# Linear ReLU attention on one core: K and V four heads to a tile in place of eight

## Chip, core and metric

The kernel runs on one NeuronCore of a Trainium2 chip. The metric is device time in microseconds, the median over several executions of the same program. One more execution was taken with the hardware profiler; its own time stands beside its span below, and every duration in this document comes from such a profiled execution.

The engines are named as in the profile: PE (TensorE, with its weight loads as PEld), DVE (VectorE), ACT (ScalarE), POOL (GpSimd) and SP (SyncE). Loads that turn float32 into bfloat16 are issued by POOL, plain transfers by SP and ACT; all of them run on the same 16 DMA engines.

## What is computed

Batch 8, 12 heads, sequence 512, head size 64, everything float32 in HBM (96 heads in all, 12.58 MB for each of Q, K, V and the output).

```python
Q_feat = np.maximum(0, Q)
K_feat = np.maximum(0, K)
KV = np.einsum('bhkd,bhkv->bhdv', K_feat, V)
K_sum = np.sum(K_feat, axis=2)
numerator = np.einsum('bhqd,bhdv->bhqv', Q_feat, KV)
denominator = np.einsum('bhqd,bhd->bhq', Q_feat, K_sum)
return (numerator / (denominator[:, :, :, None] + 1e-10)).astype(np.float32)
```

Each head first reduces K and V to a 64x64 matrix `KV` (with `K_sum` as a 65th column), and then every row of Q is multiplied by it and divided by its denominator.

## The kernel before, in words

**Tiling.** Eight heads make an octet (`o`, 0 to 11). Q and the output of an octet are 1 MB of float32 each, 128 partitions of 32 rows, so one head lies on 16 partitions. In octets 1 to 10, K and V are laid out the same way: one 1 MB load for K and one for V (`load_kv`, lines 99 to 105), 8 KB of float32 for each partition. The step number `g` = 2·o + i then means half of each partition's rows (16 of 32), of all eight heads. Octets 0 and 11 (`by4`, line 37) use another layout: there `g` means four of the eight heads, 32 partitions to a head, 16 rows to a partition, and each K or V load is 512 KB (`load_kv4`, lines 93 to 97; for octet 0 lines 112 to 116, float32, by SP and ACT).

**Keeping heads apart.** One matmul contracts over all 128 partitions, so the heads that share them are kept apart by masks. `prep(g)` (lines 171 to 186) writes K twice, times a mask for even and for odd heads (`kf`, two DVE instructions that also do the ReLU), and V once for each pair of heads (`vo`). With eight heads there are four pairs, so V is written four times (`NT = 4`): three on DVE and one on ACT for an even `g`, two and two for an odd one. With four heads there are two pairs: one copy on DVE, one on ACT. A 65th column of `vo`, set once for each buffer (`ones8`, `ones4`), holds ones in the partitions of the pair and gives `K_sum`.

**K times V.** `mm_kv(g)` (line 188) runs 16 matmuls, one for each row of a partition, with 128 columns of `kf` as weights and 260 columns of `vo` moving (four pairs of 65), or 130 with four heads. With eight heads the two steps of an octet add into one PSUM tile, and `evac_kv` (line 200) copies it on ACT after the second step, in four copies of 64x260 into `kvd`. With four heads each step has its own PSUM tile and four copies of 64x130.

**Q.** `qt(o)` transposes the octet's Q on PE (16 transposes) and ACT writes it back with the ReLU (`evac_qt`, four instructions). `out_round(o, j)`, three to an octet, multiplies it with `kvd` (`mm_out`) and DVE divides (`norm`: `den`, `rec`, `o_sb`).

**Order.** The order on every engine is written out by hand (lines 277 to 340), and each engine takes its instructions in that order. In iteration `o` of the loop: step `kv(2o)`, round 0 of octet o-1, `prep(2o+2)`, round 1, `kv(2o+1)`, `qt(o)`, `prep(2o+3)`, round 2, store of octet o-1. The last octets differ: in iteration 10 `prep(22)` stands behind all rounds of octet 9; in iteration 11 the rounds of octet 10 and its store come first, then `kv(22)`, `qt(11)`, `prep(23)`, `kv(23)`; iteration 12 is the three rounds of octet 11 and its store. Before the loop stand the masks, the fills of `vo`, `kvd` and `qt`, and `prep(0)` and `prep(1)`.

**Loads and stores.** POOL issues all loads from octet 1 on in one row (lines 125 to 130): K, V, Q of octets 1 to 10, then K and V of step 22, Q of octet 11, K and V of step 23. A load waits until its buffer is free (four octets of K and of V, seven of Q); it also waits for the landing of the load eight places before it, since POOL's loads share eight semaphores. SP issues the stores. A store of octet `o` up to 6 is held back by tiny transfers into `scratch` (lines 268 to 272), which wait until K of octet o+5 has landed (for octets 0 to 3 also V of octet o+4).

Of the kernel before, what the change touches and what calls it, by code (L numbers as in the profile page):

```python
# [10 lines left out]
def kernel(  # L11
# [7 lines left out]
    nc = tc.nc  # L19
    B, H, S, D = Q.shape  # L20
    assert D == 64
    P = 128
    D1 = D + 1
    NH = B * H

    RQ = S * 8 // P
    R = RQ // 2  # L30
    U = RQ // 2
    NT = 4
    NO = NH // 8
    assert NO * 8 == NH and RQ == 32
    DELAY = 5

    def by4(g):
        return g // 2 in (0, NO - 1)


    fp32 = mybir.dt.float32
    bf16 = mybir.dt.bfloat16
# [3 lines left out]
    def pool(name, bufs, **kw):  # L46
        return ctx.enter_context(tc.tile_pool(name=name, bufs=bufs, **kw))

    consts = pool("consts", 1)
    qin = pool("qin", 7)  # L50
    kin = pool("kin", 4)
    vin = pool("vin", 4)
    kfp = pool("kfp", 3)
    rcp = pool("rcp", 4)
    outp = pool("outp", DELAY + 2)
    pkv = pool("pkv", 2, space=bass.MemoryType.PSUM)
# [3 lines left out]
    def view(X, f):  # L60
        return X.rearrange("b h s d -> (b h s d)").rearrange("(n p f) -> n p f", p=P, f=f)

    Qr, Kr, Vr, Or = view(Q, RQ * D), view(K, RQ * D), view(V, RQ * D), view(out, RQ * D)
    Kg, Vg = view(K, R * D), view(V, R * D)

    ident = consts.tile([P, P], bf16, name="ident")
    NB = 3
    NK = 3
    NZ = 2

    vof = [consts.tile([P, R * NT * D1], bf16, name=f"vo{i}") for i in range(NB)]
    vo = [x.rearrange("p (r t d) -> p r t d", r=R, t=NT) for x in vof]
    vo4 = [x.rearrange("p (q r t d) -> p q r t d", q=2, r=R, t=2) for x in vof]
    kvf = [consts.tile([P, NT * 4 * D1], bf16, name=f"kvd{i}") for i in range(NK)]
    kvd = [x.rearrange("p (t s c d) -> p t s c d", t=NT, s=2, c=2) for x in kvf]
    mask_s = consts.tile([P, 2], fp32, name="mask_s")
    mask_h = consts.tile([P, 2, NT], fp32, name="mask_h")  # L80
    mask_t = consts.tile([P, NT], fp32, name="mask_t")
    mask4 = consts.tile([P, 2, 2], fp32, name="mask4")
    scratch = consts.tile([1, 2 * NO, D], bf16, name="scratch")


# [4 lines left out]

    q_sb, k_sb, v_sb = {}, {}, {}

    def load_kv4(g):
        k_sb[g] = kin.tile([P, R, D], bf16, name="k4_sb")
        nc.gpsimd.dma_start(out=k_sb[g].rearrange("p r d -> p (r d)"), in_=Kg[g])
        v_sb[g] = vin.tile([P, R, D], bf16, name="v4_sb")
        nc.gpsimd.dma_start(out=v_sb[g].rearrange("p r d -> p (r d)"), in_=Vg[g])

    def load_kv(o):
        k = kin.tile([P, 2, R, D], bf16, name="k_sb")  # L100
        nc.gpsimd.dma_start(out=k.rearrange("p i r d -> p (i r d)"), in_=Kr[o])  # L101
        v = vin.tile([P, 2, R, D], bf16, name="v_sb")
        nc.gpsimd.dma_start(out=v.rearrange("p i r d -> p (i r d)"), in_=Vr[o])  # L103
        for i in range(2):
            k_sb[2 * o + i], v_sb[2 * o + i] = k[:, i], v[:, i]

    def load_q(o):
        q_sb[o] = qin.tile([P, U, 2 * D], bf16, name="q_sb")
        nc.gpsimd.dma_start(out=q_sb[o].rearrange("p u f -> p (u f)"), in_=Qr[o])  # L109


    for g in range(2):
        kv = outp.tile([P, 2, R, D], fp32, name="kv_first", tag="o_sb")
        k_sb[g], v_sb[g] = kv[:, 0], kv[:, 1]
        nc.sync.dma_start(out=k_sb[g].rearrange("p r d -> p (r d)"), in_=Kg[g])
        nc.scalar.dma_start(out=v_sb[g].rearrange("p r d -> p (r d)"), in_=Vg[g])
    load_q(0)

    nc.gpsimd.memset(mask_h, 1.0)
    for base, mult, lo in ((0, 1, -16), (15, -1, 16)):  # L120
        nc.gpsimd.affine_select(
            out=mask_h, in_=mask_h, pattern=[[lo, 2], [2 * lo, NT]], compare_op=Alu.is_ge,
            fill=0.0, base=base, channel_multiplier=mult)
    make_identity(nc, ident)
    for o in range(1, NO - 1):
        load_kv(o)
        load_q(o)
    load_kv4(2 * NO - 2)
    load_q(NO - 1)
    load_kv4(2 * NO - 1)  # L130

    def masks4():
        for h in range(4):
            for s in range(2):
                nc.vector.memset(mask4[32 * h:32 * h + 32, 0, s:s + 1], 1.0 if h % 2 == s else 0.0)
        for t in range(2):
            nc.vector.memset(mask4[:, 1, t:t + 1], 0.0)
            nc.vector.memset(mask4[64 * t:64 * t + 64, 1, t:t + 1], 1.0)

    def masks8():  # L140
        nc.vector.memset(mask_t, 0.0)
        for t in range(NT):
            nc.vector.memset(mask_t[32 * t:32 * t + 32, t:t + 1], 1.0)
        nc.vector.tensor_reduce(out=mask_s, in_=mask_h, op=Alu.add, axis=mybir.AxisListType.X)


    def ones8(i):
        nc.vector.memset(vo[i][:, :, :, D:D1], 0.0)
        for t in range(NT):
            nc.vector.memset(vo[i][32 * t:32 * t + 32, :, t, D:D1], 1.0)  # L150

    def ones4(i):
        for q in range(2):
            nc.vector.memset(vo4[i][:, q, :, :, D:D1], 0.0)
            for t in range(2):
                nc.vector.memset(vo4[i][64 * t:64 * t + 64, q, :, t, D:D1], 1.0)

    def zero_kv(i):
        nc.vector.memset(kvf[i].bitcast(fp32), 0.0)  # L159

    def zero_q(i):
# [1 line left out]

    kf, ps_kv, ps_qt, ps_out = {}, {}, {}, {}

    def v_buf(g):
        return vo4[NB - 1][:, g % 2] if by4(g) else vo[(g - 2) % NB]

    def prep(g):
        ms, mt, nt = (mask4[:, 0], mask4[:, 1], 2) if by4(g) else (mask_s, mask_t, NT)
        kf[g] = kfp.tile([P, R, 2, D], bf16, name="kf")
        for s in range(2):
            nc.vector.tensor_scalar(kf[g][:, :, s, :], k_sb[g], scalar1=0.0,  # L175
                                    scalar2=ms[:, s:s + 1], op0=Alu.max, op1=Alu.mult)
        split = 1 if by4(g) else NT - 1 - g % 2
        for t in range(split):
            nc.vector.tensor_scalar(v_buf(g)[:, :, t, 0:D], v_sb[g],  # L179
                                    scalar1=mt[:, t:t + 1], scalar2=None, op0=Alu.mult)  # L180

        def on_scalar():
            for t in range(split, nt):
                nc.scalar.activation(v_buf(g)[:, :, t, 0:D], v_sb[g], Act.Copy,  # L184
                                     scale=mt[:, t:t + 1])
        return on_scalar

    def mm_kv(g):
        first, last, nt = (True, True, 2) if by4(g) else (g % 2 == 0, g % 2 == 1, NT)
        if first:  # L190
            ps_kv[g] = pkv.tile([P, NT, D1], fp32, name="ps_kv")
        else:
            ps_kv[g] = ps_kv[g - 1]
        for r in range(R):
            nc.tensor.matmul(  # L195
                ps_kv[g][:, 0:nt], kf[g][:, r, :, :].rearrange("p s d -> p (s d)"),
                v_buf(g)[:, r, :, :], start=(first and r == 0), stop=(last and r == R - 1),
                skip_group_check=True)

    def evac_kv(g):  # L200
        if by4(g):
            t0, nt = g % 2 * 2, 2
        elif g % 2 == 1:
            t0, nt = 0, NT
        else:
            return
        for s in range(2):
            for c in range(2):
                nc.scalar.copy(kvd[g // 2 % NK][64 * c:64 * c + 64, t0:t0 + nt, s, c, :],  # L209
                               ps_kv[g][64 * s:64 * s + 64, 0:nt])  # L210


    def transp(o, i):
# [13 lines left out]
    def mm_out(o, j):  # L227
        po = pou.tile([P, 2, 512], fp32, name="ps_out")
        ps_out[o, j] = po
        u0, nu = ROUNDS[j]  # L230
        for v in range(nu):
            u, b, c = u0 + v, v // (nu // 2), v % (nu // 2) * 2 * D1
            for z in range(2):
                for w in range(4):
                    hs = slice(32 * w, 32 * w + 32)
                    nc.tensor.matmul(  # L236
                        po[hs, b, c:c + 2 * D1],
                        qtf[o % NZ][:, z, u * P + 32 * w:u * P + 32 * w + 32],
                        kvd[o % NK][:, w, z, :, :],
                        start=(z == 0), stop=(z == 1), skip_group_check=True)  # L240

    def norm(o, j, o_sb):
# [31 lines left out]
        for ps, rs in cuts(o):  # L274
            nc.sync.dma_start(out=Ov[ps, rs], in_=o_sb[ps, rs])

    masks4()
    ones4(NB - 1)
    prep(0)()
    zero_kv(0)  # L280
    prep(1)()
    zero_q(0)
    masks8()
    ones8(0)
    ones8(1)
    zero_kv(1)
    zero_kv(2)
    zero_q(1)
    def kv(g):
        mm_kv(g)  # L290
# [13 lines left out]
    for o in range(NO + 1):  # L304
        if o > 0:
            o_sb = outp.tile([P, RQ, D], fp32, name="o_sb", tag="o_sb")
        if o < NO - 2:
            kv(2 * o)
            if o > 0:
                out_round(o - 1, 0, o_sb)  # L310
            if o == 1:
                ones8(NB - 1)
            prep(2 * o + 2)()
            if o > 0:
                out_round(o - 1, 1, o_sb)
            kv(2 * o + 1)
            qt(o)
            prep(2 * o + 3)()
            if o > 0:
                out_round(o - 1, 2, o_sb)  # L320
                store(o - 1, o_sb)
            continue
# [8 lines left out]
        if o < NO:  # L331
            g = 2 * o + 2 if o == NO - 2 else 2 * o + 1
            if o == NO - 1:
                kv(2 * o)
                qt(o)
            if o == NO - 2:
                ones4(NB - 1)
            prep(g)()
            if o == NO - 1:
                kv(g)  # L340
# [28 lines left out]
```

## Time and profile before

| what | value |
|---|---|
| three runs, us | 134.3, 135.56, 136.13 (median 135.56) |
| the profiled execution's own time | 136.13 us |
| its span, first to last instruction | 134.4 us |
| PE busy, weight loads (PEld) busy | 91.5 us (68%), 76.0 us (57%) |
| DVE busy | 93.5 us (70%) |
| ACT busy | 81.5 us (61%) |
| POOL busy | 22.0 us (16%) |
| HBM read, written | 37.75 MB, 12.58 MB |
| queue q0 (POOL's loads) | 5184 packets, 17.83 MB as landed, 66.5% of 16 engines |
| queue q1 (SP: stores and the first K) | 2544 packets, 13.63 MB, 25.8% of 16 engines |
| granted TensorE clock, mean | 0.917 |

The 1.73 us between the span and the execution's own time lie outside the first and last instruction. Bytes of POOL's loads are counted as they land, in bfloat16; the same load reads twice as much from HBM. A packet of such a load is one partition's share: 8 KB read and 4 KB written with the 1 MB loads, half of that with the 512 KB loads.

### The profile page before, as it was taken

What the parts mean: (1) busy time and instruction counts of PE and PEld (TensorE: products, weight loads), DVE (VectorE), ACT (ScalarE), POOL (GpSimd) and SP (SyncE); (2) the same over time, 40 slices, a digit from 0 to 9 for tenths busy, and PEclk for the clock granted to TensorE, in tenths of its full rate; (3) what the DMA queues carried; (4) which work ended last, traced back from release to release, by engine and by line L of the source; (5) the groups of instructions that cost most, each with busy time, mean ns of one, the idle gap of its engine ahead of it and who ended that gap; (6) DMA issues with size and microseconds to landing.
All of it is one profiled execution on the core that took longest, in us unless ns stands there. A gap on an engine that the chain in (4) does not pass through costs nothing.

```text
span 134.4 us, 4829 instructions
## 1 busy us (share of the span) xinstructions
PE 91.5 (68%) x2112; PEld 76.0 (57%) x2112; DVE 93.5 (70%) x260; ACT 81.5 (61%) x139; POOL 22.0 (16%) x45
## 2 busy tenths in 40 slices
PE   0043802997779697891997997949989765756740
PEld 0052702686568586781686886838776654645720
DVE  2347679169997996969835989989598717930280
ACT  0246296319929779695079697985979467084200
POOL 6911311220401310411110410220000000000000
PEclk9999995599999999999599999999999999686577
DMA  4999999999999999999999999999999999980015
GB/s 101 371 307 210 215 211 215 215 213 212 217 211 216 213 265 299 216 285 287 216 289 291 213 282 288 222 287 295 211 307 266 237 383 413 395 351 24 5 79 233
DMA packets 8036, 32.81 MB, mean 244 GB/s; under 512 B 1232, under 2 KB 1232, under 8 KB 6608
## 3 DMA queue, kind: packets, MB, share of 16 engines
q0 software_dynamic: 5184, 17.83, 66.5%
q1 hardware_dynamic: 2544, 13.63, 25.8%
q10 hardware_dynamic: 288, 1.05, 2.1%
q8 instruction: 16, 0.26, 0.7%
q14 instruction: 4, 0.03, 0.1%
HBM read 37.75 MB, written 12.58 MB: 374 GB/s over the span
## 4 chain that ended last, share of the span: by engine, by line
PE 36%; ACT 24%; DVE 19%; issue 11%; DMA 7%; SPq 0%; ACTq 0%; DVEq 0%
PE ps_kv L195 24%; PE ps_out L236 9%; ACT vo L184 9%; ACT qt L222 8%; ACT kvd L209 7%; DMA kv_first<-in_K_dram 7%; DVE o_sb L249 5%; DVE kf L175 3%; DVE vo L179 3%; PE ps_qt L216 3%; DVE qt L162 3%; DVE rec L248 1%; DVE kvd L159 1%; DVE den L246 1%; DVE vo L150 1%
## 5 line engine op out<-in xcount | busy, mean ns | idle before, releaser
L195 PE MATMUL ps_kv<-vo,kf 128*128 128x260 bf16 (+1 forms) x384 | 50.5, 293 | 25.4 <-ACT vo L184 15.3
L195 PEld LDWEIGHTS <-kf 128*128 128x128 bf16 x384 | 38.1, 109 | 34.0 <-DVE vo L179 16.9
L236 PE MATMUL ps_out<-kvd,qt 128*32 128x130 bf16 x1536 | 31.5, 231 | 12.3 <-issue 8.8
L209 ACT CAST kvd<-ps_kv 64x260 bf16<-64x260 f32 (+1 forms) x56 | 19.2, 342 | 31.2 <-PE ps_kv L195 30.6
L184 ACT ACTIVATE vo<-v_sb,mask_t 128x1024 bf16<-128x1024 bf16 x30 | 33.2, 1187 | 4.0 <-DMA v_sb<-in_V_dram 4.0
L236 PEld LDWEIGHTS <-qt 128*32 128x32 bf16 x1536 | 24.9, 101 | 18.7 <-issue 12.2
L249 DVE TENSOR_TENSOR o_sb<-ps_out,rec 128x768 f32<-128x768 f32 (+1 forms) x36 | 31.3, 869 | 1.2
L222 ACT ACTIVATE qt<-ps_qt 128x512 bf16<-128x512 bf16 x48 | 24.8, 603 | 0.3
L246 DVE TENSOR_SCALAR den<-ps_out 128x12 f32<-128x12 f32 (+1 forms) x36 | 5.9, 163 | 24.1 <-PE ps_out L236 24.1
L179 DVE TENSOR_SCALAR vo<-v_sb,mask_t 128x1024 bf16<-128x1024 bf16 x50 | 21.5, 482 | 0.0
L175 DVE TENSOR_SCALAR kf<-k_sb,mask_s 128x1024 bf16<-128x1024 bf16 x40 | 17.4, 478 | 0.0
L216 PE MATMUL ps_qt<-ident,q_sb 128*128 128x128 bf16 x192 | 14.1, 232 | 0.0
L216 PEld LDWEIGHTS <-q_sb 128*128 128x128 bf16 x192 | 13.1, 106 | 0.4
L103 POOL DMA_DIRECT2D v_sb<-in_V_dram x10 | 5.6, 557 | 25.3 <-ACT vo L184 13.7
L109 POOL DMA_DIRECT2D q_sb<-in_Q_dram x12 | 7.4, 617 | 13.4 <-DMA k_sb<-in_K_dram 7.8
L101 POOL DMA_DIRECT2D k_sb<-in_K_dram x10 | 5.8, 584 | 21.4 <-DMA q_sb<-in_Q_dram 9.2
L248 DVE RECIPROCAL rec<-den 128x12 f32<-128x12 f32 (+1 forms) x36 | 7.9, 220 | 1.2
L175 DVE TENSOR_SCALAR kf<-kv_first,mask 128x1024 bf16<-128x1024 f32 x4 | 2.8, 751 | 4.9 <-DMA kv_first<-in_K_dram 4.9
L184 ACT ACT_TABLE_LOAD x1 | 1.3, 1283 | 5.9 <-DMA kv_first<-in_V_dram 5.9
L162 DVE MEMSET qt<- 128x2048 f32 x2 | 3.5, 1765 | 0.8 <-issue 0.8
L184 ACT ACTIVATE vo<-kv_first,mask 128x1024 bf16<-128x1024 f32 x2 | 2.4, 1178 | 2.5 <-DMA kv_first<-in_V_dram 2.5
L184 ACT ACTIVATE vo<-v_sb,mask 128x1024 bf16<-128x1024 bf16 x2 | 2.4, 1197 | 0.0
(24 smaller groups left out, 12.4 us busy)
## 6 DMA issues: line engine op xcount, KB each, us to landing
out_dram<-o_sb SPq DMA_DIRECT2D x9, 1024.0 KB, 9.2
q_sb<-in_Q_dram POOLq DMA_DIRECT2D x12, 512.0 KB, 21.7
k_sb<-in_K_dram POOLq DMA_DIRECT2D x10, 512.0 KB, 21.2
v_sb<-in_V_dram POOLq DMA_DIRECT2D x10, 512.0 KB, 20.8
out_dram<-o_sb SPq DMA_DIRECT2D x2, 896.0 KB, 9.6
kv_first<-in_V_dram ACTq DMA_DIRECT2D x2, 512.0 KB, 5.1
kv_first<-in_K_dram SPq DMA_DIRECT2D x2, 512.0 KB, 4.9
out_dram<-o_sb SPq DMA_DIRECT2D x2, 512.0 KB, 2.8
```

What stands on the lines that cost most here:

```text
L109: nc.gpsimd.dma_start(out=q_sb[o].rearrange("p u f -> p (u f)"), in_=Qr[o])
L162: nc.vector.memset(qtf[i].rearrange("p z f -> p (z f)").bitcast(fp32), 0.0)
L175: nc.vector.tensor_scalar(kf[g][:, :, s, :], k_sb[g], scalar1=0.0, scalar2=ms[:, s:s + 1], op0=Alu.max, op1=Alu.mult)
L179: nc.vector.tensor_scalar(v_buf(g)[:, :, t, 0:D], v_sb[g], scalar1=mt[:, t:t + 1], scalar2=None, op0=Alu.mult)
L184: nc.scalar.activation(v_buf(g)[:, :, t, 0:D], v_sb[g], Act.Copy, scale=mt[:, t:t + 1])
L195: nc.tensor.matmul(ps_kv[g][:, 0:nt], kf[g][:, r, :, :].rearrange("p s d -> p (s d)"), v_buf(g)[:, r, :, :], start=(first and r == 0), sto ...
L209: nc.scalar.copy(kvd[g // 2 % NK][64 * c:64 * c + 64, t0:t0 + nt, s, c, :], ps_kv[g][64 * s:64 * s + 64, 0:nt])
L216: nc.tensor.transpose(ps_qt[o, i][:, u, :], q_sb[o][:, i * (U // 2) + u, :], ident)
L222: nc.scalar.activation(qtz[o % NZ][:, z, us, :, z, :], pv[:, :, :, z, :], Act.Relu)
L236: nc.tensor.matmul(po[hs, b, c:c + 2 * D1], qtf[o % NZ][:, z, u * P + 32 * w:u * P + 32 * w + 32], kvd[o % NK][:, w, z, :, :], start=(z == ...
L248: nc.vector.reciprocal(rec, den)
L249: nc.vector.tensor_tensor(o_sb[:, 2 * u0:2 * (u0 + nu)].rearrange("p (b r) d -> p b r d", b=2), pv[:, :, :, 0:D], rec.unsqueeze(3).to_broa ...
```

## The change

Octets 1 to 10 take the layout that octets 0 and 11 already have. Every step `g` is now four heads; `load_kv(g)` loads 512 KB of K and 512 KB of V, so POOL issues 22 loads of each in place of 10 large and 2 small ones. `NT`, `by4`, `load_kv4`, `masks8`, `ones8`, `ones4` and the POOL instructions that made `mask_h` go. V is written twice in each step (one copy on DVE, one on ACT). Every step has its own PSUM tile of 2x65 columns and its own four copies into a `kvd` buffer of half the size; there are four `vo` and four `kvd` buffers in place of three. K and V have twelve buffers of 512 KB each as loaded (six octets in place of four), `kf` four in place of three. The loop's order, the rounds, the stores and the order of the last octets' loads stay; the stores' `scratch` transfers now wait for the first half of K of octet o+5.

```diff
-    NT = 4
+    NHG = 4
-    def by4(g):
-        return g // 2 in (0, NO - 1)
...
-    kin = pool("kin", 4)
-    vin = pool("vin", 4)
-    kfp = pool("kfp", 3)
+    kin = pool("kin", 12)
+    vin = pool("vin", 12)
+    kfp = pool("kfp", 4)
...
-    NB = 3
-    NK = 3
+    NB = 4
+    NK = 4
...
-    def load_kv(o):
-        k = kin.tile([P, 2, R, D], bf16, name="k_sb")
-        nc.gpsimd.dma_start(out=k.rearrange("p i r d -> p (i r d)"), in_=Kr[o])
...
+    def load_kv(g):
+        k_sb[g] = kin.tile([P, R, D], bf16, name="k_sb")
+        nc.gpsimd.dma_start(out=k_sb[g].rearrange("p r d -> p (r d)"), in_=Kr[g])
+        v_sb[g] = vin.tile([P, R, D], bf16, name="v_sb")
+        nc.gpsimd.dma_start(out=v_sb[g].rearrange("p r d -> p (r d)"), in_=Vr[g])
...
     for o in range(1, NO - 1):
-        load_kv(o)
+        load_kv(2 * o)
+        load_kv(2 * o + 1)
         load_q(o)
-    load_kv4(2 * NO - 2)
+    load_kv(2 * NO - 2)
     load_q(NO - 1)
-    load_kv4(2 * NO - 1)
+    load_kv(2 * NO - 1)
...
+    def zero(i):
+        if i == 0:
...
+        if i < NB:
+            nc.vector.memset(vo[i][:, :, :, D:D1], 0.0)
+            for t in range(2):
+                nc.vector.memset(vo[i][64 * t:64 * t + 64, :, t, D:D1], 1.0)
         nc.vector.memset(kvf[i].bitcast(fp32), 0.0)
...
-        split = 1 if by4(g) else NT - 1 - g % 2
-        for t in range(split):
-            nc.vector.tensor_scalar(v_buf(g)[:, :, t, 0:D], v_sb[g],
-                                    scalar1=mt[:, t:t + 1], scalar2=None, op0=Alu.mult)
...
+        nc.vector.tensor_scalar(vo[g % NB][:, :, 0, 0:D], v_sb[g], scalar1=mask[:, 1, 0:1],
+                                scalar2=None, op0=Alu.mult)
+
+    def prep_act(g):
+        nc.scalar.activation(vo[g % NB][:, :, 1, 0:D], v_sb[g], Act.Copy, scale=mask[:, 1, 1:2])
 
     def mm_kv(g):
-        first, last, nt = (True, True, 2) if by4(g) else (g % 2 == 0, g % 2 == 1, NT)
...
+        ps_kv[g] = pkv.tile([P, 2, D1], fp32, name="ps_kv")
         for r in range(R):
             nc.tensor.matmul(
...
+                ps_kv[g], kf[g][:, r, :, :].rearrange("p s d -> p (s d)"), vo[g % NB][:, r, :, :],
+                start=(r == 0), stop=(r == R - 1), skip_group_check=True)
 
     def evac_kv(g):
...
         for s in range(2):
             for c in range(2):
-                nc.scalar.copy(kvd[g // 2 % NK][64 * c:64 * c + 64, t0:t0 + nt, s, c, :],
-                               ps_kv[g][64 * s:64 * s + 64, 0:nt])
+                nc.scalar.copy(kvd[g % NK][64 * c:64 * c + 64, :, s, c, :],
+                               ps_kv[g][64 * s:64 * s + 64])
...
-                        kvd[o % NK][:, w, z, :, :],
+                        kvd[(2 * o + h // 4) % NK][:, h % 4 // 2, h % 2, :, :],
...
-    masks4()
-    ones4(NB - 1)
-    prep(0)()
-    zero_kv(0)
-    prep(1)()
+    zero(0)
+    prep(0)
+    prep_act(0)
+    zero(1)
+    prep(1)
+    prep_act(1)
     zero_q(0)
-    masks8()
-    ones8(0)
-    ones8(1)
-    zero_kv(1)
-    zero_kv(2)
+    for k in range(2, NK):
+        zero(k)
     zero_q(1)
...
-            if o == 1:
-                ones8(NB - 1)
...
-            if o == NO - 2:
-                ones4(NB - 1)
```

## Prediction, made before the changed kernel ran

> **What bounds the kernel now.** I read the page first: its slices, then its chain.
>
> ```profile
> DMA  4999999999999999999999999999999999980015
> ...
> PE 36%; ACT 24%; DVE 19%; issue 11%; DMA 7%; SPq 0%; ACTq 0%; DVEq 0%
> ```
>
> Two things look binding at once. The DMA engines are full from the second slice to about 120 us, yet the chain that ended last holds almost no DMA: its 7% are the first K. So the loads arrive ahead of their use, and the engines' own order sets the end. The chain in order of time shows one octet in the middle:
>
> ```profile
> 69.94 1.57 ACT qt L222 x3
> 71.51 2.11 ACT vo L184 x2
> ...
> 73.67 1.97 PE ps_kv L195 x16
> ...
> 77.70 1.57 ACT qt L222 x3
> ```
>
> From `qt` to `qt` is 77.70 - 69.94 = 7.76 us: the Q write on ACT, two V copies, 16 matmuls of K times V, and four copies of `kvd` from 75.6 to 77.2 (left out above). That ring is the compute pace; stalls of PE (the "issue" gaps, up to 3 us) come on top: the transposes of octet 1 start at 29.6 us and those of octet 11 at 117.8, 8.8 us an octet.
>
> How far ahead are the loads? The answer for POOL's line 97 (V of steps 22 and 23) and the chain at the end tell:
>
> ```profile
> L97 POOL DMA_DIRECT2D v_sb<-in_V_dram x2: 527/586/645, 79.6 to 90.1; - x2
> ...
> DMA to landing us min/median/max: 24.4/24.5/24.7
> ```
>
> ```profile
> 121.18 1.06 ACT vo L184
> ```
>
> The very last V is issued at 90.1 and lands 24.4 us later, at 114.5. Its ACT copy starts at 121.0 (1.20 long; the chain counts its last 1.06). So 6.5 us pass between landing and use. The same sum for V of octet 10 (issued 73.9, 22.7 to landing, so 96.6; the ACT copy of step 21 starts at 103.6) gives 6.9. Behind the last V copy, from 122.2 to 134.4, come 12.2 us that the diff leaves alone: matmul, copies, three rounds, store.
>
> **Start.** Between the two fills of `qt` DVE spends 14.6 to 18.8 on `masks8`, two `ones8` and two `kvd` fills, 4.2 us. After, two `zero` calls stand there: each a 128x32 fill, two 64x16 fills and half a `kvd` fill, about 0.75 with gaps, 1.5 in all. Another stands between `prep(0)` and `prep(1)`, where DVE waited 2.05 us for K anyway. `prep(2)` starts 2.7 us earlier, and its first matmuls waited for exactly that DVE work. Loads don't prevent it: ACT's wait for V of octet 1 ended at 15.8.
>
> **Each octet on the engines.**
>
> ```profile
> L184 ACT ACTIVATE vo<-v_sb,mask_t 128x1024 bf16<-128x1024 bf16 x30 | 33.2, 1187 | 4.0 <-DMA v_sb<-in_V_dram 4.0
> L179 DVE TENSOR_SCALAR vo<-v_sb,mask_t 128x1024 bf16<-128x1024 bf16 x50 | 21.5, 482 | 0.0
> L209 ACT CAST kvd<-ps_kv 64x260 bf16<-64x260 f32 x40 | 15.0, 374 | 24.4 <-PE ps_kv L195 24.1
> L209 ACT CAST kvd<-ps_kv 64x130 bf16<-64x130 f32 x16 | 4.2, 263 | 6.7 <-PE ps_kv L195 6.5
> ```
>
> - ACT: 3 V copies become 2 (-1.19), 4 x 374 ns become 8 x 263 ns (+0.61): -0.58. With the Q write (4 x 603) 7.47 becomes 6.89.
> - DVE: 5 V copies become 2: -1.45, of about 8.1 (4 `kf` at 478, 5 `vo`, 3.76 for the rounds).
> - PE: 32 matmuls as before, half the moving columns. 16 of 260 columns take 1.95 at full clock; 16 of 130 took 1.89 to 1.92, but at half clock. The nearest full-clock row is 16 transposes of 128 columns, 1.05. So 0 to 0.9 less for a step; I take 0.9, since the transposes too went from 1.91 to 1.05.
>
> After, ACT's own 6.9 is the shortest ring: at least 0.58, at most 0.87 less for an octet. By octet 10 that is 2.7 + 9 x 0.58 = 7.9 us, more than the 6.9 by which its V lay waiting. Compute catches the loads, and the rest of the gain has nowhere to go: what is late next is landing.
>
> **Landing.** Total bytes stay, and DMA is full, so landing moves only by what the smaller packets cost. Two stretches of the DMA view compare them: large loads alone (36 to 42 us), and a mixture with hardly a store (105 to 107). In each, the first line is all traffic and the q0 line POOL's loads: packets, MB as landed, share of 16 engines.
>
> ```profile
> DMA packets 346, 1.28 MB, mean 213 GB/s; under 512 B 37, under 2 KB 37, under 8 KB 345
> ...
> q0 software_dynamic: 345, 1.26, 105.0%
> ```
>
> ```profile
> DMA packets 218, 0.43 MB, mean 213 GB/s; under 512 B 51, under 2 KB 51, under 8 KB 213
> ...
> q0 software_dynamic: 184, 0.38, 100.2%
> ```
>
> In the second, q1 had 33 packets of 0.03 MB, four stores of 8 KB and 29 small marks, so of the 51 small ones 22 are q0's; its other 162 packets make 0.38 MB if about 138 are half-size, 74% of the bytes. The rate of all traffic is the same 213: price 0. By engine time for each MB of q0, 16 x 6 x 1.05 / 1.26 = 80.0 against 16 x 2 x 1.002 / 0.38 = 84.4, 5.5% more at 74%. K and V of octets 1 to 10 are 20 MB at about 2.5 us each, 49 us, so the upper end is 49 x 0.055 / 0.74 = 3.6 us. I take 1.3, nearer to the rate, which is what landing follows; but 0.05 MB of the second stretch were no loads, so not 0. Below zero has no reason: bytes are equal.
>
> [...]
>
> POOL issues 20 more loads at 0.56: 11 us on an engine busy 22 of 134, in the shadow of transfers it waits for. Eight in flight now hold 4.8 MB, some 12 us of transfer; an issue takes 0.6. Buffers no longer hold it up. SP's stores wait for the first half of K of octet o+5, about 2.5 us earlier in the load order; the last six see the same K of step 22 (issued 76.8, 26.1 to landing: 102.9) as before, and the loads behind it are unchanged in size, so the final 114.5 - 102.9 = 11.6 us of loading repeat.
>
> **Can ACT be ready at the last landing?** When V of step 21 lands (96.6), ACT has at most 4 `kvd` copies, the Q write and the V copy ahead of it: 1.1 + 2.1 + 1.2, so it is through at 101.0 instead of 105.8. From there to readiness for the last V copy took 121.0 - 105.8 = 15.2; less 0.9 (matmul), 0.4 (copies of step 21), 1.1 (`ones4`, on the chain at 111.4 to 112.6), plus 1.1 for copies of step 20: 13.9, so 114.9, against 114.5 + 1.3 = 115.8. It is close, so I add 0.5 (bounds 0 and 1.5) for PE stalls and a slow clock.
>
> What a pause does to PE is in two stretches:
>
> ```profile
> 60.00:64.00 4.00, 1.11 (x77) 0.93 (x65) 3.33 (x8) 2.25 (x3) 0.53 (x1) 1.00 1.05 286
> 64.00:67.50 3.50, 3.41 (x19) 2.36 (x20) 2.94 (x7) 0.00 (x0) 0.89 (x2) 0.54 1.06 213
> ```
>
> PE pauses 3 us, and the granted clock behind it is 0.54. With PE waiting for landings this will come more often. [...] PE's octet at half clock is 2 x 1.9 + 1.9 + about 3.5 of rounds, 9.2, still under the 10 us between octets' landings, so it costs only near the end.
>
> **The sum.** 114.5 + 1.3 (packets) + 0.5 (readiness) + 1.2 (V copy) + 12.2 (tail) = 129.7 for the span; plus 1.7 outside, 131.4 for the profiled execution, whose before was 136.13. The median before is 135.56, so 131.4 x 135.56 / 136.13 = 130.9.
>
> **Rivals.**
> - Compute stays behind the loads (0.17). PE at half clock and its stalls stretch the ring by as much as it loses, and only the start is gained: 135.56 - 2.7 = 132.9, range 132 to 136. For it: the stalls, 11% of the chain. Against: DVE and ACT both lose work.
> - Slower: each smaller load costs a pause on the slowest DMA engine, since a landing needs all 16 and POOL's next issue waits for a landing (0.20). With a price p for each of 20 added loads the last V lands 20p later; from p = 0.33 us the 6.5 us in hand are gone. At 0.5 it is 135.6 + 10 - 6.5 = 139. For it: K and V of step 22, half-size, landed 1.4 apart (V: 79.6 + 24.7), against half of 2.5, though a store ran beside them. Against: the equal rate of 213.
> - The change doesn't do what its words say (0.05): the order of the last octets, loads included, is already that of before, and no gain comes from there; if the cover I see is not real either, 135.6.
> - The forecast (0.58): 128 to 133.
>
> **Numbers.** 130.9. The range 128.0 to 137.5 leaves out the upper part of the slower case (0.15) and some 0.04 below. About 2% is what a measurement here tells from no change, so faster means under 132.8, slower over 138.3. Faster: 0.56 of the forecast and 0.07 of the first rival, 0.63; slower 0.15; the rest, 0.22, within.
>
> **What would show it.** The last ACT V copy should follow a landing at once, with its idle time ended by the DMA of V, and the chain should hold that DMA, its start near 116. Issue plus time to landing of the last V tells the packet price; rows of 130 columns at full clock tell PE's share; `prep(2)` should start near 17.8. I am wrong if the last V lands after 121, or if ACT reaches it long after it landed.

## The result, and the profile after

| | before | after |
|---|---|---|
| median of 6 runs, us | 135.66 (133.97 to 136.13) | 129.29 (128.54 to 129.51) |
| profiled execution, its span | 136.13, 134.4 | 129.49, 127.7 |
| ratio, 95% interval | | 0.9562 [0.9498, 0.9626] |

Here and below a ratio with its interval is taken from the undisturbed executions alone and a median from all, so the two need not fit each other (in e5 two of four executions count as disturbed, the profiled one among them).

The page of after, with the rows that answer to those of before: the slices of DMA, the chain that ended last (shares by engine, and the DMA among its lines above), and the groups that the change touched.

```profile
DMA  3999999999999999999999999999999999999835
...
DMA 49%; PE 23%; DVE 11%; issue 9%; ACT 4%; SPq 0%; ACTq 0%; POOLq 0%
...
L149 ACT CAST kvd<-ps_kv 64x130 bf16<-64x130 f32 x96 | 25.3, 264 | 22.3 <-PE ps_kv L142 20.3
L137 ACT ACTIVATE vo<-v_sb,mask 128x1024 bf16<-128x1024 bf16 x22 | 26.1, 1186 | 10.2 <-DMA v_sb<-in_V_dram 9.9
...
L133 DVE TENSOR_SCALAR vo<-v_sb,mask 128x1024 bf16<-128x1024 bf16 x22 | 10.7, 484 | 3.4 <-DMA v_sb<-in_V_dram 3.4
```

The chain has turned over: 49% of it is DMA, 7% before. Its part at the end, in order of time (start, length, what):

```profile
95.29 19.09 DMA v_sb<-in_V_dram
114.38 0.02 issue
114.40 1.19 ACT vo L137
115.59 0.04 issue
115.63 1.86 PE ps_kv L142 x16
```

And ACT's timeline at the same place (start, length, line and operation, in brackets the idle time before it and what ended it):

```profile
111.22 2.06 ACT L162 ACTIVATE qt<-ps_qt 128x512 bf16<-128x512 bf16 x4
114.40 1.18 ACT L137 ACTIVATE vo<-v_sb,mask 128x1024 bf16<-128x1024 bf16 x1 [1.11 <-DMA v_sb<-in_V_dram]
```

The last V lands at 114.38 and is copied at once; ACT had been idle for 1.11 us. Before, the last V landed at 114.5 and its copy began at 121.04. So the last copy begins 6.64 us earlier, which is the whole difference of the profiled executions (136.13 - 129.49 = 6.64). Compute has caught the loads. The question that is left is where it made up 6.64 us, for the middle of the kernel doesn't show it:

| | before | after | earlier by |
|---|---|---|---|
| first transposes of octet 3 | 47.5 | 41.3 | 6.2 |
| of octet 7 | 83.2 | 74.1 | 9.1 |
| of octet 10 | 108.6 | 102.5 | 6.1 |

From octet 3 to octet 10 it is 61.1 us before and 61.2 after. The lead was there by octet 3; what came on top of it by octet 7 was lost again, and seven lighter octets added nothing. Yet the engines did get less to do, as the busy times from 39 to 113 us show (length; PE, PEld, DVE, ACT, POOL busy with instructions; clock; DMA; GB/s), first of before, then of after:

```profile
39.00:113.00 74.00, 60.97 (x1532) 50.57 (x1531) 58.77 (x154) 56.82 (x96) 10.05 (x17) 0.98 1.06 268
```

```profile
39.00:113.00 74.00, 52.32 (x1499) 45.65 (x1490) 51.91 (x128) 51.93 (x117) 15.67 (x29) 0.88 1.09 266
```

ACT has 4.9 us less to do, DVE 6.9, PE 8.7, and about as many matmuls pass PE. The saved time is there, but as idle time.

### The profile page after: what moved, and what is told of

The parts are those of the page before. It is cut to its first block, busy times and chain, and to the rows that moved or that the text cites. A ratio compares the mean times of both kernels' runs of the same rounds, so it can differ in the third digit from the quotient of the medians.

```text
span 127.7 us, 4879 instructions
## 1 busy us (share of the span) xinstructions
PE 79.5 (62%) x2112; PEld 69.8 (55%) x2112; DVE 80.7 (63%) x210; ACT 77.6 (61%) x169; POOL 31.4 (25%) x62
## 4 chain that ended last, share of the span: by engine, by line
DMA 49%; PE 23%; DVE 11%; issue 9%; ACT 4%; SPq 0%; ACTq 0%; POOLq 0%
DMA v_sb<-in_V_dram 42%; PE ps_out L177 10%; PE ps_kv L142 10%; DMA kv_first<-in_K_dram 7%; PE ps_qt L156 3%; DVE o_sb L190 3%; DVE qt L124 3%; DVE kf L131 2%; ACT vo L137 2%; ACT kvd L149 1%; ACT qt L162 1%; DVE vo L133 1%; DVE rec L189 1%; DVE kvd L121 0%; DVE den L187 0%
## 5 line engine op out<-in xcount | busy, mean ns | idle before, releaser
L142 PE MATMUL ps_kv<-vo,kf 128*128 128x130 bf16 x384 | 33.6, 253 | 23.1 <-ACT vo L137 13.1
L177 PE MATMUL ps_out<-kvd,qt 128*32 128x130 bf16 x1536 | 35.2, 248 | 17.5 <-issue 15.7
L142 PEld LDWEIGHTS <-kf 128*128 128x128 bf16 x384 | 28.4, 114 | 26.6 <-DVE vo L133 18.4
L177 PEld LDWEIGHTS <-qt 128*32 128x32 bf16 x1536 | 28.2, 110 | 23.2 <-issue 19.1
L149 ACT CAST kvd<-ps_kv 64x130 bf16<-64x130 f32 x96 | 25.3, 264 | 22.3 <-PE ps_kv L142 20.3
L137 ACT ACTIVATE vo<-v_sb,mask 128x1024 bf16<-128x1024 bf16 x22 | 26.1, 1186 | 10.2 <-DMA v_sb<-in_V_dram 9.9
L85 POOL DMA_DIRECT2D k_sb<-in_K_dram x22 | 12.3, 557 | 36.2 <-DMA q_sb<-in_Q_dram 13.2
L131 DVE TENSOR_SCALAR kf<-k_sb,mask 128x1024 bf16<-128x1024 bf16 x44 | 19.4, 482 | 2.3 <-DMA k_sb<-in_K_dram 2.3
L87 POOL DMA_DIRECT2D v_sb<-in_V_dram x22 | 12.2, 554 | 17.5 <-DMA k_sb<-in_K_dram 6.1
L133 DVE TENSOR_SCALAR vo<-v_sb,mask 128x1024 bf16<-128x1024 bf16 x22 | 10.7, 484 | 3.4 <-DMA v_sb<-in_V_dram 3.4
L91 POOL DMA_DIRECT2D q_sb<-in_Q_dram x12 | 6.5, 542 | 10.4 <-DMA v_sb<-in_V_dram 4.0
```

What stands on the lines that cost most here:

```text
L133: nc.vector.tensor_scalar(vo[g % NB][:, :, 0, 0:D], v_sb[g], scalar1=mask[:, 1, 0:1], scalar2=None, op0=Alu.mult)
L137: nc.scalar.activation(vo[g % NB][:, :, 1, 0:D], v_sb[g], Act.Copy, scale=mask[:, 1, 1:2])
L142: nc.tensor.matmul(ps_kv[g], kf[g][:, r, :, :].rearrange("p s d -> p (s d)"), vo[g % NB][:, r, :, :], start=(r == 0), stop=(r == R - 1), s ...
L149: nc.scalar.copy(kvd[g % NK][64 * c:64 * c + 64, :, s, c, :], ps_kv[g][64 * s:64 * s + 64])
L177: nc.tensor.matmul(po[hs, b, c:c + 2 * D1], qtf[o % NZ][:, z, u * P + 32 * w:u * P + 32 * w + 32], kvd[(2 * o + h // 4) % NK][:, h % 4 // ...
```

## The experiments

**First: which part of the change made the lead.** The theory was the prediction's, a shorter ring of ACT, DVE and PE in every octet; the rivals, the start alone and the matmuls' columns alone. e1 gives each engine its V copies of before back, into a spare tile; e2 the 260 moving columns; e3 both. e4 asks the other question, on the kernel before: what do loads of half the size cost by themselves?

```diff
 e1, e3: in prep (DVE) and prep_act (ACT), octets 1 to 10
+        for _ in range(2 - g % 2):
+            nc.vector.tensor_scalar(spare[:, :, 0, 0:D], v_sb[g], ...)
...
+        if g % 2 == 1:
+            nc.scalar.activation(spare[:, :, 1, 0:D], v_sb[g], ...)
 e2, e3: in mm_kv, w = 2 in octets 1 to 10
-                ps_kv[g], kf[g][:, r, :, :]..., vo[g % NB][:, r, :, :],
+                ps_kv[g][:, 0:w], kf[g][:, r, :, :]..., vo[g % NB][:, r:r + w, :, :],
 e4: in load_kv of the kernel before
+        for i in range(2):
+            cols = slice(i * R * D, (i + 1) * R * D)
+            nc.gpsimd.dma_start(out=k[:, i]..., in_=Kr[o][:, cols])
+            nc.gpsimd.dma_start(out=v[:, i]..., in_=Vr[o][:, cols])
```

> The changed kernel, with as many V copies in octets 1 to 10 as before (three more on DVE and one more on ACT for each octet, written to a spare tile). Theory (less preparation lets compute catch the loads, and the last landing then sets the end at 129.3): ACT's ring grows from 6.9 to 8.1 us, compute falls behind the loads again, the last V's ACT copy starts some us after its landing at about 114.4; 130.5 to 134.5. Rival (the gain came with the transfers: smaller loads, six octets of buffers in place of four): unchanged, 128.7 to 129.9.

> The changed kernel with 260 moving columns in the K times V matmuls of octets 1 to 10 (each matmul also multiplies the next row; the second half of its output is not used). Theory: PE has room between landings, 129.0 to 130.3, last V's copy still right at its landing. Rival (PE's halved columns made the gain): 131 to 135.

> Both of the two above: the V copies and the 260 columns back, second half of the output not used; smaller loads, deeper buffers and the shorter start stay. Theory: as much work as before on every engine, so 132 to 136, the last V waiting some 4 us or more after its landing. Rival (transfers, buffers): 128.7 to 129.9.

> The kernel before, with each 1 MB load of K and of V issued as two of 512 KB (half of each partition's row), in the order K, V, K, V. Theory: the size costs nothing and compute sets the end: 134.5 to 136.5, last V landing at 113.5 to 115.5. Rival (a price of 0.33 us or more for each of 20 added loads): last V lands at 121 or later, 136 to 142.

Measured, all four on one chip: e1 128.94 us, ratio 0.949 [0.9409, 0.9571]; e2 130.68, 0.9607 [0.9522, 0.9692]; e3 132.33, 0.9728 [0.9639, 0.9818]; e4 135.51, 1.0004 [0.994, 1.0068].

e1 is the miss that matters: the V copies, from which the prediction drew an octet's gain on ACT and DVE, cost nothing as extra work in the loop. But the extra copies stand behind those that PE waits for, so e1 and e3 don't undo what fewer copies give ahead of the first matmuls of octet 1. e2's interval overlaps that of after; in its trace the last copy starts at 116.0, 2.15 us behind its landing (113.85), so the columns do count a little. Some 0.5 us of that lie at the start, in fills of the wider `vo` that e2 needs (`prep(2)` starts at 18.99, in after at 18.51). With both (e3) it starts 4.4 behind (113.43, 117.81), which is more than the two by themselves: what a delay costs depends on how much is left of the 1.1 us in hand. e4 takes as long as before with 20 more loads, but that doesn't settle the price of the packets: in its one trace the last V landed at 117.17, 2.6 us later than in before and outside the expected 113.5 to 115.5, hidden by a compute that came at 121.4 anyway. More is told by the kernels with the whole change: in after, e1, e2 and e3 the last V lands at 113.4 to 114.4, no later than the 114.5 of before.

**Second: the start, the buffers, smaller loads.** e5 delays DVE by ten spare fills before its second fill of `qt`, e6 does so in e3. In the trace of e5 the fills take 3.84 us, gaps included, and `prep(2)` starts at 21.79, 3.3 us later than in after and 1.3 later than in before. e7 takes the deeper buffers back. e8 halves the loads of after once more, to 256 KB.

```diff
 e5, e6: before the loop
     for k in range(2, NK):
         zero(k)
+    for _ in range(10):
+        nc.vector.memset(spare_f, 0.0)
     zero_q(1)
 e7
-    kin = pool("kin", 12)
-    vin = pool("vin", 12)
+    kin = pool("kin", 8)
+    vin = pool("vin", 8)
 e8: in load_kv, X = Kr and Vr
+            for i in range(2):
+                rows, cols = slice(i * R // 2, (i + 1) * R // 2), slice(i * R * D // 2, (i + 1) * R * D // 2)
+                nc.gpsimd.dma_start(out=x[g][:, rows]..., in_=X[g][:, cols])
```

> The changed kernel with ten fills of a spare tile (10 x 0.275 = 2.75 us of DVE) in front of the second fill of qt, so that octet 1 starts as late as before. Theory (landing sets the end, compute has time in hand): 128.7 to 130.0, last V copied right at its landing. Rival (the shorter start makes a good part of the gain): 131 to 132.5.

> The run with all work of octets 1 to 10 back (V copies and 260 columns; part of the products unused), which took 132.33, with the late start of e5 as well. Left of the change: smaller loads, six octets of buffers, a PSUM tile and copies for each step, no fills between octets 10 and 11. Theory (what is left is the order of the copies and the fills): 132.5 to 134.5. Rival (the start is the rest of the gain): 135 to 136.5.

> The changed kernel with eight buffers of K and of V (four octets, as before) in place of twelve. Theory (DMA is full either way, so landing stays): 128.7 to 130.0. Rival (deeper buffers bring the loads earlier): 131 to 135.

> The changed kernel with each load of K and of V issued as two of 256 KB (2 KB read and 1 KB landed for each partition), 44 loads more; the stores wait for the second half. Theory (a smaller packet costs little): last V lands at 114 to 116.5, 129 to 131.5. Rival (0.33 us or more for each added load): last V lands at 128 or later, 143 or more.

Measured: e5 132.10 us, 0.9649 [0.9502, 0.9796]; e6 133.97, 0.9887 [0.9792, 0.9983]; e7 129.11, 0.9489 [0.9403, 0.9575]; e8 139.51, scattered from 134.37 to 142.75, so no ratio is given.

e7: the deeper buffers do nothing. e8: the price of small loads, not to be seen at 512 KB, is large at 256 KB: even in the profiled execution (134.37) the last V lands at 119.13, 4.75 later than in after, for 44 more loads, or 0.11 us a load; that lies between its two expectations, and both missed. e5's interval overlaps that of after, but all of its executions (130.05 to 132.72) lie above all of e7's on the same chip (127.80 to 129.35), and its trace shows where the delay stays: the last copy starts 2.6 us later than in after. This contradicts what "compute catches the loads" suggested: most of a delay at the start isn't absorbed on the way but stands to the end. Something paces PE at nearly the same rate whether ACT and DVE carry much or little.

**Where PE stands still.** The waits of after name it (engine and line, what it waited for: total, times, longest): "issue", time in which PE waited for nothing that the profile shows.

```profile
PEld L177 <- issue: 19.1, 15, 3.5
PE ps_out L177 <- issue: 15.7, 9, 3.3
```

In before the first of these rows had 12.2 us in 13 pauses:

```profile
PEld L236 <- issue: 12.2, 13, 3.2
```

PE's timeline of after over two of the pauses:

```profile
46.02 1.40 PE L177 MATMUL ps_out<-kvd,qt 128*32 128x130 bf16 x83 [1.65 <-issue]
47.35 1.11 PE L142 MATMUL ps_kv<-vo,kf 128*128 128x130 bf16 x16
48.30 1.05 PE L156 MATMUL ps_qt<-ident,q_sb 128*128 128x128 bf16 x16
49.28 0.41 PE L177 MATMUL ps_out<-kvd,qt 128*32 128x130 bf16 x13
52.21 0.47 PE L177 MATMUL ps_out<-kvd,qt 128*32 128x130 bf16 x19 [2.52 <-issue]
```

From pause to pause are 83 + 16 + 16 + 13 = 128 matmuls, each with its weight load: 256 instructions. The second pause cuts an output round in two (13 matmuls ahead of it, 19 behind), where no operand changes hands. Numbering all PE rows of after by start, the pauses over 0.8 us between 20 and 110 us begin at these rows:

```
row    449   705   1217  1473  1729  2241  2497  2753  3265  3777
us     27.4  33.8  46.0  52.2  58.5  71.3  77.3  83.5  95.7  107.9
idle   0.96  2.69  1.65  2.52  3.33  1.47  2.43  1.48  2.53  1.78
```

All are 449 plus a multiple of 256. And the DMA view of after, from 20 to 116 us, has a queue that carries instructions (packets, MB, share of 16 engines):

```profile
q8 instruction: 15, 0.25, 0.9%
```

One packet of 16 KB for each 256 PE rows. A packet starts some 3.7 us after PE entered the block ahead of it (3.5 to 4.1 in after), takes about 0.95, and where PE has paused it goes on about 1.4 after the packet's end. At row 1473: the block before was entered at 46.02, the packet ran from 49.86 to 50.74, PE went on at 52.21. That is some 6.1 us for 256 PE instructions; the twelve blocks from row 705 to row 3777 of after took 5.8 to 7.0 each, 6.18 on the mean. An octet has 32 + 16 + 128 = 176 matmuls, 352 instructions or 1.375 blocks: 8.5 us, more than the 6.9 of ACT's ring after, and more than the 7.76 before.

The period of 256 rows, the one packet of 16 KB for each and the restart behind its end say together that PE's instructions are fetched in blocks of 256. The profile doesn't name the engine that a q8 packet serves, so this is the author's reading of the trace, which e9 and e12 put to the test. The time at the block edges from row 449 to row 3777 in which PE neither multiplies nor loads weights adds up to 22.2 us in after, and to 10.4 in before. Between these two rows, the edges at the ends left out, 19.5 of the 20.4 us of PE's pauses over 0.15 us in after stand at block edges, in before 8.5 of 14.1.

**Third: fewer instructions.** If the fetch sets the pace, the kernel before should run faster with fewer PE instructions, at all its old work on ACT and DVE. e9 does its output rounds with half the matmuls, each of 260 columns, and leaves out the products of odd heads: 224 PE instructions to an octet.

```diff
-            for z in range(2):
-                for w in range(4):
+            for w in range(4):
...
-                        po[hs, b, c:c + 2 * D1],
-                        qtf[o % NZ][:, z, ...],
-                        kvd[o % NK][:, w, z, :, :],
-                        start=(z == 0), stop=(z == 1), ...)
+                    po[hs, b, c:c + 4 * D1],
+                    qtf[o % NZ][:, 0, ...],
+                    kvd[o % NK][:, w, :, :, :],
+                    start=True, stop=True, ...)
```

> The kernel before, with half as many matmuls in the output rounds, each moving 260 columns instead of 130: the products of the second half of the weights (z = 1) are left out, PE's streaming time stays, and an octet takes 224 PE instructions in place of 352 (a matmul and its weight load are two). All V copies, kvd copies and norms stay. Theory now (PE is held by the fetch of its instructions, 256 in at least 6.1 us while DMA is full, which all runs so far show from the third octet on): the pace falls from 8.5 to the ring of 7.8 us an octet, compute meets the landings, 128.5 to 132. Rival (the ring of ACT and DVE sets the pace of before, as the prediction had it; PE's pauses only happen beside it): 134.5 to 136.5.

Measured: 132.64 us (132.05 to 133.04), ratio 0.9779 [0.9719, 0.984], a gain with as many moving columns in fewer instructions, and a little less of it than expected (the time lies 0.6 us above the theory's range, outside the rival's). Octets 3 to 7 start at 45.96, 53.73, 61.49, 69.25 and 77.02: 7.76 or 7.77 apart each time, the ring of ACT as the prediction had read it. The same window of e9 as above, with its 990 matmuls:

```profile
39.00:113.00 74.00, 58.92 (x990) 46.35 (x988) 62.02 (x161) 56.74 (x95) 10.20 (x17) 0.99 1.06 270
```

PE is as busy as in before (58.9 us against 61.0), but the pauses are fewer: ten q8 packets from 20 to 116 us in place of 14. It stops at 132.6 because compute then meets the landings. Its chain in order of time shows the place:

```profile
69.52 26.65 DMA v_sb<-in_V_dram
96.25 1.18 ACT vo L184
```

V of octet 10 lands at 96.2, and from there the eight-head order needs 21 us to the last V copy at 117.13. In after the same V lands at 97.2 and ACT is ready for the last copy at 113.3, 16.1 us later; probably because a step of four heads can begin with half of an octet's V, which no run separates.

**Also: is there more to be had?** e10 and e11 start from after. Both move the fills of `qt` from DVE to POOL, to start earlier, and hold the stores back, so that loads have the DMA engines to themselves for longer: the `scratch` transfers wait for Q of octet o+5 (e10) or o+6 (e11).

```diff
         load_kv(2 * o)
+        if o == 2:
+            for x in qtf:
+                nc.gpsimd.memset(x..., 0.0)
         load_kv(2 * o + 1)
...
-        n = 2 * (o + DELAY)
-        if n < 2 * NO:
-            for x, i in ((v_sb, n - 1), (k_sb, n))[0 if o < 4 else 1:]:
-                nc.sync.dma_start(out=scratch[:, i], in_=x[i][0:1, 0, :])
+        n = o + DELAY
+        if n < NO:
+            nc.sync.dma_start(out=scratch[:, n], in_=q_sb[n][0:1, 0, 0:D])
```

> The changed kernel with the two fills of qt on POOL while it waits for its ninth load (off DVE, in front of prep of step 2), and each store up to octet 6 held until Q of octet o+5 has landed, in place of K. Theory now (the start plus the fetch's pace set when compute is ready, the stores between the loads set when the last V lands): first fetch about 4 us earlier, ready near 109.5, last V landed at 110 to 112, 124.5 to 127.5. Rival (only the last landing counts and DMA is full in any case): 128 or more.

> As e10, with the stores held until Q of octet o+6 has landed. Theory now: last V lands at 105 to 108, compute is ready near 109.5 and ends near 122, and the stores left over end it: 124 to 127.5. Rival as for e10: 128 or more.

Measured: e10 128.50 us, 0.948 [0.9418, 0.9542]; e11 128.83, 0.9497 [0.944, 0.9554]. Both miss their aim and land where the rival said, at 128 or more; their intervals overlap that of after (0.9498 to 0.9626), so neither is shown to be better. The last V does land earlier, at 111.03 and 108.42, against 114.38. In e10 ACT then gets to it only at 112.24, paced by PE again. In e11 the copy starts at 109.05 and the divisions are done at 118.6, but the store issued at 118.61 lands only at 125.32, behind the backlog: what was taken from the stores' share is due at the end.

**Fourth: more instructions.** The test that could have sunk the theory: after, with one more matmul of a single column behind each of the K times V matmuls of octets 1 to 10, into a spare column of PSUM. It leaves no work out, but what it computes is not the attention above. It adds 64 instructions to an octet (416) and hardly any work.

```diff
+            if 2 <= g < 2 * NO - 2:
+                nc.tensor.matmul(
+                    ps_kv[g][:, 2, 0:1], kf[g][:, r, :, :]...,
+                    vo[g % NB][:, r, 0, 0:1], start=True, stop=True, ...)
```

> The changed kernel with one more matmul of a single column behind each of the 16 of K times V in octets 1 to 10, into a spare PSUM column: 32 matmuls or 64 PE instructions more in an octet, 416 in place of 352, and about as much more PE time (a weight load of 128 columns each, some 0.9 us a step) as the wider columns of e2 added. Theory now (PE gets 256 instructions in at least 6.1 us): an octet takes 416 / 256 x 6.15 = 10.0 us in place of 8.5, 1.5 us more over some nine octets, 139 to 145. Rival (PE's time or the engines' ring counts, not the number of instructions): as e2, 129.5 to 132.

Measured: 141.64 us (140.54 to 142.48), ratio 1.0513 [1.0376, 1.0651]. The window of e12, and that of e2:

```profile
39.00:113.00 74.00, 55.12 (x1570) 49.78 (x1570) 43.99 (x108) 46.38 (x103) 16.03 (x29) 0.82 1.09 266
```

```profile
39.00:113.00 74.00, 59.92 (x1547) 49.47 (x1546) 50.57 (x126) 50.99 (x114) 15.69 (x29) 0.98 1.08 266
```

e2 gives PE more work in the same number of instructions and takes 130.68; e12 gives it more instructions with hardly any work in them and takes 141.64. PE is less busy in e12, and DVE and ACT get less done in the 74 us (108 and 103 instructions against 126 and 114). In before, after, e2 and e12 some 1,500 to 1,570 matmuls pass in 74 us, however long each is. From row 705 to row 3777 the blocks of e12 took 6.08 us on the mean, which makes 416 / 256 x 6.08 = 9.9 us an octet, against 352 / 256 x 6.18 = 8.5 in after. From the transposes of octet 1 to those of octet 10 it is 9.8 us an octet in e12 (25.90 to 114.33); single octets scatter widely, as a pause falls into them or not.

## Why the prediction was right, and where its reasons were not

The time (130.9 predicted, 129.29 measured), the sign and the state at the end are as forecast. The terms of the sum:

| term | predicted | measured in after |
|---|---|---|
| last V lands | 114.5 + 1.3 for packets = 115.8 | 114.38 |
| wait of ACT behind the landing | 0.5 | 0.02 |
| V copy | 1.2 | 1.18 |
| from there to the end of the span | 12.2 | 127.7 - 115.58 = 12.1 |
| outside the span | 1.7 | 1.79 |

The whole error lies in two allowances, 1.3 for the packets and 0.5 for readiness, both within their bounds (0 to 3.6, 0 to 1.5) and both zero here. The packets' rate read from two stretches of the trace was a better sign for after than the engine time for each MB, though e4's trace, with its landing 2.6 us later, leaves a doubt; e8 shows that it may not be carried to half that size again. That the landing would be late next, near the old 114.5, was right, as was the cover: ACT was ready at 113.29, where the prediction had 114.9. Less right was that "the final 114.5 - 102.9 = 11.6 us of loading repeat": K of step 22 landed at 104.72, 1.8 us later than in before, and the last V only 9.7 us behind it. That the two nearly cancel was luck.

**The step that failed is the pace.** "That ring is the compute pace; stalls of PE (the 'issue' gaps, up to 3 us) come on top", and from it "at least 0.58, at most 0.87 less for an octet ... 2.7 + 9 x 0.58 = 7.9 us". The ring was rightly read, and e9 runs at it once the fetch is out of the way. But the stalls didn't come on top: they are a second pace, 8.5 us an octet by instruction count, which the change leaves as it is. The times of two block edges, twelve blocks apart:

| | PE row 705, us | PE row 3777, us | between | last V lands | its copy starts |
|---|---|---|---|---|---|
| before | 39.11 | 113.95 | 74.84 | 114.5 | 121.04 |
| after | 33.76 | 107.94 | 74.18 | 114.38 | 114.40 |
| e1, V copies back | 33.80 | 107.49 | 73.69 | 114.00 | 114.02 |
| e2, columns back | 35.69 | 110.54 | 74.85 | 113.85 | 116.00 |
| e3, both back | 36.32 | 111.15 | 74.83 | 113.43 | 117.81 |
| e5, late start | 36.78 | 110.25 | 73.47 | 114.12 | 116.98 |
| e6, both and late | 39.88 | 113.41 | 73.53 | 114.28 | 118.61 |

Twelve blocks are 8.7 octets; at 0.58 they should have become 5 us shorter, and became 0.7 shorter. Of the 6.64 us, 5.35 had been won before row 705, that is by the transposes of octet 2, 0.66 came in the twelve blocks and 0.63 behind them. What is put back shows in the time of row 705 (e2 1.9 us later than after, e3 2.6, e5 3.0, e6 6.1); in the twelve blocks behind it no kernel of the table gains or loses more than some 0.7 us on after. For each packet follows PE's entry into a block (3.5 to 4.1 us behind it in after, 3.2 to 4.7 in before), so the whole row of packets moves with the first: it starts at 24.87 in after, 28.41 in e5, 29.78 in before.

- **Start.** `prep(2)` begins at 18.5 after and 20.5 before: 2.0 of the 2.7 promised. The first matmuls of octet 1 begin 2.8 us earlier (19.73, 22.55), since two V copies fewer stand ahead of them on DVE. That the start would still count at the end was right, but for a wrong reason: not because compute caught the loads octet by octet, but because the blocks behind it neither add to a lead nor take much of it.
- **Columns.** "16 of 130 took 1.89 to 1.92, but at half clock", so 0 to 0.9 less: at full clock they take 1.11 us (the timeline above), 0.84 less. But only the steps at the start kept their gain. The first matmuls of octet 1 took 2.1 us less (the lines below, before and then after); the granted clock was low in both (0.50 from 22.5 to 26.2 us in before, 0.63 from 19.7 to 21.4 in after), so not all of it is owed to the columns (with 260 columns e2 took 3.23 at the same place, e7 with 130 took 1.92).

```profile
22.55 3.65 PE L195 MATMUL ps_kv<-vo,kf 128*128 128x260 bf16 x16 [6.41 <-DVE vo L179]
```

```profile
19.73 1.59 PE L142 MATMUL ps_kv<-vo,kf 128*128 128x130 bf16 x16 [3.49 <-DVE vo L133]
```

- **V copies.** -0.58 on ACT and -1.45 on DVE for an octet are there as busy time (56.8 to 51.9 and 58.8 to 51.9 in the window) and, past the first matmuls of octet 1, brought nothing (e1).
- **The stretch from 60 to 67.5 us of before,** which the prediction showed for the half clock, was a block edge: a q8 packet ran from 61.61 to 62.48 and PE went on at 64.09 with row 1729. The pause was seen, and its period wasn't asked for. After, such pauses are longer, and the mean clock from 39 to 113 us falls from 0.98 to 0.88; with PE waiting at the block edges anyway no cost of that shows, but no run separates it.
- **POOL.** Its 20 more issues are there (31.4 us busy, 22.0 before), and no cost of them shows, as put down.
- **The rivals.** "Compute stays behind the loads" failed by 1.1 us, the time ACT had in hand: e5, 3.3 us later at the start, is that rival, at 132.10. "Each smaller load costs a pause" doesn't show at 512 KB with eight in flight (the last V of after lands at 114.38); at 256 KB the loads do cost time (e8), by what way wasn't traced.

What stays open: why an instruction packet starts only 3.7 us after PE entered the block ahead of it. In the traces the 16 engines are full (busy share 1.06 to 1.09 from 39 to 113 us in before, after, e2, e5, e9 and e12); no kernel was run with them idle, so whether it queues behind the loads' packets or would take as long alone wasn't separated. Nor is it known why e4's last V landed 2.6 us later in its trace and that of after didn't.

## What to carry to other kernels

Before crediting a change with time saved in a loop, look at PE's "issue" pauses and count the instructions from one to the next. In after it was a multiple of 256 each time (pauses over 0.8 us), weight loads counted. Fewer instructions made an octet shorter (e9, 224 in place of 352: 7.76 us in place of 8.9 from octet 3 to octet 7), while lighter ones turned into idle time (PE busy 52.3 of 74 us in after, 61.0 in before). A head start before such a loop was kept here to its last block within 0.7 us, so a microsecond in the prologue may be worth more than one in every turn of the loop. And two paces lay close together here (7.8 and 8.5 us), and the profile of before showed some octets 7.76 us apart and others 8.2 to 12.4; taking the shortest for the pace and the rest for accidents is the error made here.

## What the runs showed of the hardware

- In after every pause of PE over 0.8 us between 20 and 110 us stood at the edge of a block of 256 instructions, weight loads counted, with one 16 KB instruction packet for each block on the DMA engines that also carry the data (15 packets, 0.9% of the 16 engines from 20 to 116 us in after). With these full, blocks took 6.1 to 6.2 us on the mean of twelve (6.18 in after, 6.24 in before), single ones 4.5 to 8.7 (the two extremes both in e1), with pauses of up to 3.3 us in after and 3.6 in e11. The mean is longer in e4 (6.4) and e8 (6.6).
- With loads that turn float32 into bfloat16 at 512 KB in place of 1 MB the last one landed no later (114.38 in after, 114.53 in before; 117.17 in e4), at 256 KB 4.75 us later (e8), so here the price near zero of one halving told nothing of the next.
- Beside a fill on POOL a DVE instruction took longer. In e10 POOL's two fills of `qt` ran from 6.11 to 9.73 us, and the two `kf` instructions of DVE, together 1.42 us in after, took 5.37:

```profile
5.56 5.37 DVE L134 TENSOR_SCALAR kf<-kv_first,mask 128x1024 bf16<-128x1024 f32 x2 [3.02 <-DMA kv_first<-in_K_dram]
```

In e11, which has the same edit, they took 5.36. So the 3.5 us of fills taken off DVE's list brought `prep(2)` only 2.5 us forward (16.02 in e10 and e11, 18.51 in after).
